# The units of an input projection in another order, and the two halves of an attention tile in one

## The chip, the cores and the metric

The kernel runs on one core of a Trainium2 chip. The metric is the device time of one execution in microseconds. Before the change three runs gave 1636.99, 1639.19 and 1640.86 us, with a median of 1639.19.

## The reference

One decoder layer is computed for two groups of requests with shared weights: a prompt of 1024 positions and 8 sample sequences of 8 positions, 1088 columns together, d_model 1024, in FP32. Cut to what matters here:

```
proj = rmsnorm(x) @ w_in        # q | k | v | glu_a | glu_b | gate_a | gate_b
A = sliding_window_attention(q, k, v) @ w_o_attn       # window 128, sinks
u = glu_a * sigmoid(glu_b)                             # 1024 channels
c = depthwise_conv(u, 31 taps) + bias
B = silu(layernorm(c)) @ w_pb
h = x + (sigmoid(gate_a) * A + sigmoid(gate_b) * B) @ w_out
y = h + conv_ffn(rmsnorm(h))
```

The change lies wholly in the second of three lines of work: the projection `proj`, the attention and the convolution `c`, which run side by side. The LayerNorm begins at their end.

## The kernel before

Activations are held with channels on the 128 partitions and the 1088 columns along the free axis, in chunks of 384, 384 and 320. FP32 products are made of three `fp32r` matmuls: each operand is split in a high part (a cast) and a low part (the rest), and `mm3` (lines 207 to 210) adds high by high, high by low and low by high. The whole stretch from 71 us to about 640 us is one long stream of such matmuls on PE.

**Units.** A unit is one tile of 128 output channels: three chunks of 8 times 3 matmuls. `SEQUENCE` (line 62) writes down their order: `b` is glu_b of the next channel tile, `a` glu_a of the same tile, `g` the next of 16 gate tiles, `q0`, `k0`, `q1`, `k1` the tiles of queries and keys for the two halves of the heads, `v` the two halves of the values (both are used in one unit of 9 blocks, 128x256 each). `weight_order` (line 92) turns it into the order in which weights are read, and `phase_x` (line 730) walks along it. The units are called below by letter and count from zero: a.7 is glu_a of the last of eight tiles, g.15 the last gate tile. The first five (b a g g g) are written apart and are the same before and after.

**Weights.** `weight` (line 196) issues the load of the raw weights two units ahead (`wraw`, on SP), and the split one unit ahead: ACT casts `whi` (L179), ACT writes its negative to `wlo` (L180), and a DMA issued by POOL (L181) adds `wraw` to `wlo`. PE's second kind of product in a unit can begin when that DMA has landed. There are two buffers of each. For `v` a third pair lies in the tile `p` of the attention pool.

**Convolution.** `do_b` takes one of two buffers `u` (`u_start`, line 747: two memsets on POOL and a small load on SP), ACT copies the chunks of glu_b there and takes the sigmoid, `do_a` has DVE multiply the chunks of glu_a into it (L774), and `conv` (line 570) runs 15 times three multiply-adds on DVE (L582), between a sum `sm` (L590) at the start and three combining operations (L602 to L604) at the end. It is issued with `later(CONV_LATER)`, a priority that puts its operations behind others that are ready. Its result goes to DRAM (`d_c`, L605 and L606, DMAs on POOL's queue), and the buffer `u` is free when they have landed.

**Attention.** After `v` and after the last `q1` unit, `plan_units` lays the steps of eight attention units and four sample units out over ticks (a tick is one k step of a unit): `scores` (L449, L450 on PE; copies, mask L454, softmax), `turn` (four transposes L461, then a split of the result in `pth` and `ptl` by ACT and DVE, L244, and two DVE multiplies by the mask, L471), and `mix` (L482 on PE with `pth`, `ptl` and their masked copies). A sample unit loads cached keys and values by DMAs on POOL's queue (`kp`, `vp`, L516 and L517).

**End of the stretch.** At the unit that stands `LAST_GATES` = 2 before the end, the agenda is drained, the pool of the attention is closed, and in its room lie `ah`, `al` (the attention's first half, six loads on SP, L1018 and L1019) and the tiles `ct` of the LayerNorm. In the last unit `ln_steps` (line 608) begins: `ct` is loaded from `d_c` for all eight channel tiles (L634), DVE sums it over the tiles (L620), and PE takes the means by a matmul with a constant (L628).

Each of SP, POOL, DVE, ACT and PE works its own instructions in the order in which the scheduler put them; the scheduler orders them when the kernel is built, by priority and by its own estimate of what is ready.

Of the kernel before, what the change touches and what calls it, by code (L numbers as in the profile page):

```python
# [6 lines left out]
F32 = mybir.dt.float32  # L7
F32R = mybir.dt.float32r
AF = mybir.ActivationFunctionType
ALU = mybir.AluOpType  # L10
AX = mybir.AxisListType

P = 128
# [12 lines left out]
WIN = 128  # L26
# [33 lines left out]
FIRST = 5  # L60
LAST_GATES = 2
SEQUENCE = (
# [3 lines left out]
).split()  # L66
OUT_TAIL = 4
LAST_WEIGHT = 153
# [61 lines left out]
class Build:  # L130
# [291 lines left out]
    def attn_unit(self, p, blk, st):  # L422
        nc = self.nc
        q, kd, kl = st["q"], st["kd"], st["kl"]
        qs = slice(blk * P, (blk + 1) * P)
        first = max(blk - 1, 0) * P
        keys = slice(first, first + 2 * WIN)
        own = slice(WIN, 2 * WIN) if blk else slice(0, WIN)
        live = [{}, {}]
        vals = {}  # L430

        def values():
            vt = vals["vt"] = self.t(self.at, [P, 2, 4, HD], "vt", F32R, bufs=2)
            self.split_ps(vt[:, 0, 0:4:3, :], vt[:, 0, 1:3, :], self.v[:, blk, p])
            if blk:
                d = self.t(self.at, [P, 2, HD], "vd")
                nc.vector.tensor_tensor(d, self.v[:, blk - 1, p], self.v[:, blk, p], ALU.subtract)
                self.split_ps(vt[:, 1, 0:4:3, :], vt[:, 1, 1:3, :], d)

        def scores(g):  # L440
            pt = live[g]["pt"] = self.t(self.at, [P, 4, WIN + 4], "p", bufs=2)
            hd = 4 * (2 * p + g)
            nc.gpsimd.tensor_copy(pt[:, :, WIN:WIN + 1], self.c("sink", hd, 4)[:, :, None])
            above = self.masks[:, 0:WIN].bitcast(mybir.dt.uint32)[:, None, :]
            for jj in range(2):
                ps = self.bank("aux").rearrange("p (a b) -> p a b", a=2)
                for j in range(2):
                    h = 2 * jj + j
                    nc.tensor.matmul(ps[:, j, :], q[g][:, h, qs], kd[g][:, keys], start=True, stop=False)  # L449
                    nc.tensor.matmul(ps[:, j, :], q[g][:, h, qs], kl[g][:, keys], start=False, stop=True)  # L450
                two = pt[:, 2 * jj:2 * jj + 2, 0:WIN]
                nc.scalar.copy(two, ps[:, :, own])
                other = ps[:, :, 0:WIN] if blk else self.least[:, None, :].to_broadcast([P, 2, WIN])
                nc.vector.copy_predicated(two, above.to_broadcast([P, 2, WIN]), other)  # L454
            self.band_softmax(pt)

        def turn(g):
            pt = live[g]["pt"]
            ps = self.bank("aux")
            for h in range(4):  # L460
                nc.tensor.transpose(ps[:, h * P:(h + 1) * P], pt[:, h, 0:P], self.ident)  # L461
            ph = self.t(self.at, [P, 512], "pth", F32R)
            pl = self.t(self.at, [P, 512], "ptl", F32R)
            parts = [(0, ph), (0, pl)]
            with self.later(TURN_SOONER if self.now - self.gated <= 3 else 0):
                self.split_ps(ph, pl, ps)
                if blk:
                    below = self.masks[:, None, WIN:2 * WIN].to_broadcast([P, 4, WIN])
                    for x, tag in ((ph, "pth0"), (pl, "ptl0")):
                        x0 = self.t(self.at, [P, 512], tag, F32R)  # L470
                        nc.vector.tensor_tensor(x0.rearrange("p (a b) -> p a b", a=4),  # L471
                                                x.bitcast(F32).rearrange("p (a b) -> p a b", a=4), below, ALU.mult)
                        parts.append((1, x0))
            live[g]["parts"] = parts

        def mix(g):
            r, o = [slice(x * HD, (x + 1) * HD) for x in (g, 1 - g)]
            av = self.bank("aux")
            parts = live[g]["parts"]
            for n, (y, x) in enumerate(parts):  # L480
                v = vals["vt"][:, y, 2 * g:2 * g + 2, :].rearrange("p x d -> p (x d)")
                nc.tensor.matmul(av, v, x, start=n == 0, stop=n == len(parts) - 1)  # L482
            if g == 0:
                live[0]["t"] = self.t(self.at, [P, 4 * P], "av").rearrange("p (a b) -> p a b", a=4)
            t = live[0]["t"]
            av = av.rearrange("p (a b) -> p a b", a=4)
            nc.scalar.copy(t[r], av[o])
            nc.vector.tensor_tensor(t[r], av[r], t[r], ALU.add)
            if g == 1:
                self.split_ps(q[0][:, :, qs], q[1][:, :, qs], t)  # L490
            if p == 0 and g == 1 and blk in (3, 7):
                b0 = (blk - 3) * P
                self.attn_spill(st, slice(b0, b0 + 4 * P))

        steps = [(A_VALUES, values)]
        for g in range(2):
            steps.append((A_SCORE[g], lambda g=g: scores(g)))
            steps.append((A_TURN[g], lambda g=g: turn(g)))
            steps.append((A_MIX[g], lambda g=g: mix(g)))
        return steps  # L500
# [229 lines left out]
    def phase_x(self):  # L730
        nc, tc, a, pool = self.nc, self.tc, self.a, self.pool
# [103 lines left out]
        def do_k(p):  # L835
            st = states[p]
            st["ks"] = self.t(kv, [P, NS], "ks")
            st["kd"] = [self.t(kv, [P, SEQ], f"kd{g}", F32R) for g in range(2)]
            st["kl"] = [self.t(kv, [P, SEQ], f"kl{g}", F32R) for g in range(2)]

            def ev(c, o, n, ps):
                m = min(n, SEQ - o)
                for g in range(2):
                    r, x = [slice(y * HD, (y + 1) * HD) for y in (g, 1 - g)]
                    kd = st["kd"][g][:, o:o + m]
                    nc.scalar.copy(kd[r], ps[r, :m])
                    kl = st["kl"][g][:, o:o + m]
                    nc.vector.tensor_tensor(kl[r], ps[r, :m], kd[r].bitcast(F32), ALU.subtract)
                    nc.scalar.copy(kd[x], ps[r, :m])
                    nc.scalar.copy(kl[x], kl[r].bitcast(F32))  # L850
                if m < n:
                    nc.scalar.copy(st["ks"], ps[:, m:n])
                    kf = self.t(gl, [P, 384], "gt", bufs=2)[:, :WIN]
                    nc.scalar.copy(kf, ps[:, m - WIN:m])
                    nc.gpsimd.dma_start(a["o_kp"][p], kf)
                    nc.gpsimd.dma_start(a["o_kn"][p], st["ks"])

            self.stream(("k", p), xs, ev)

        def do_v():  # L860
            ws = [self.weight(("v", 0)), self.weight(("v", 1))]
# [144 lines left out]
        for n, (kind, i) in enumerate(self.order[:self.n_in]):  # L1006
# [18 lines left out]
            if kind == "b":  # L1025
                u = do_b(i)
            elif kind == "a":
                do_a(i, u)
            elif kind in ("ga", "gb"):
                self.stream((kind, i), xs, gate_evac(kind, i))  # L1030
            elif kind == "q":
                if i == (1, 0):
                    self.drain()
                self.stream((kind, i), xs, q_evac(*i))
                if i == (1, 3):
                    plan_units(1)
            elif kind == "k":
                do_k(i)
            elif kind == "v":
                if i == 0:  # L1040
                    do_v()
                    plan_units(0)
# [1181 lines left out]
```

## Time and profile before

| | |
|---|---|
| profiled execution | 1639.45 us |
| its span | 1637.7 us |
| median of the runs | 1639.19 us (1636.99 to 1640.86) |
| granted TensorE clock, mean over the span | 0.998 of full speed |
| DVE, ACT, POOL busy | 84%, 55%, 18% of the span |
| ACT busy, microseconds | 901.9 |

In a row of the timeline stand the start in microseconds, the duration, the engine, the line of the kernel, the operation with its output and inputs, a count, and in square brackets how long the engine was idle ahead of it and who ended that. In a row of the waits stand the waiting engine and instruction, whom it waited for, the sum in microseconds, how often, and the longest. In a table by stretches stand, for each engine, busy microseconds and the number of instructions, then the granted TensorE clock, the busy share of the DMA engines, and GB/s. Durations of matmuls are modelled and overlap: the distance of two starts is the time that one takes.

The profile has one notable shape: PE has work nearly always, and DVE is saturated in some stages and idle in others.

### The profile page before, as it was taken

Reading aid. Unit: us, or ns where it says so; the run is one execution under the profiler, and the core shown is the slowest. Engines: PE = TensorE matmul, PEld = TensorE weight load, DVE = VectorE, ACT = ScalarE, POOL = GpSimd, SP = SyncE. Lnnn points to the kernel's source line nnn. Section 1 sums busy time; section 2 is a strip of 40 time slices with the busy share of each in tenths; the row PEclk is TensorE's granted clock in tenths of the full one; section 3 lists DMA queues with packets and bytes.
Section 4 is the critical chain, followed back from the end, with each engine's and each line's share of the span. In section 5 each row is a group of like instructions: output and inputs, shape, how many; then the busy total and the mean of one; then the engine's idle time right before and its main releaser. Section 6 shows DMA issues by size and latency. Waiting matters only on the chain.

```text
span 1637.7 us, 30023 instructions
## 1 busy us (share of the span) xinstructions
PE 1621.8 (99%) x11428; PEld 1602.6 (98%) x11428; DVE 1369.8 (84%) x2463; ACT 901.9 (55%) x1948; POOL 301.6 (18%) x587
## 2 busy tenths in 40 slices
PE   9999999999999999999999999999999999999998
PEld 9999999999999999999999999999999999999998
DVE  7889678999869996788755999988888877889767
ACT  6535387875588754576532465555555555524322
POOL 0210122333112221111102422322222111000000
PEclk9999999999999999999999999999999999999999
DMA  6343433545433366548763632344444334676423
GB/s 211 98 98 90 114 95 97 140 132 143 109 85 78 118 215 202 176 154 232 188 227 102 209 119 72 112 116 118 119 120 109 106 106 157 225 177 160 110 62 110
DMA packets 110329, 221.51 MB, mean 135 GB/s; under 512 B 26600, under 2 KB 57320, under 8 KB 110168
## 3 DMA queue, kind: packets, MB, share of 16 engines
q1 hardware_dynamic: 81528, 131.47, 26.0%
q0 software_dynamic: 28224, 87.71, 20.2%
q8 instruction: 90, 1.47, 0.4%
q14 instruction: 55, 0.45, 0.1%
q10 hardware_dynamic: 432, 0.40, 0.1%
HBM read 137.55 MB, written 64.03 MB: 123 GB/s over the span
## 4 chain that ended last, share of the span: by engine, by line
PE 80%; DVE 8%; DMA 4%; issue 4%; ACT 3%; POOL 0%; SPq 0%; POOLq 0%; DVEq 0%; ACTq 0%
PE mm L208 19%; PE mm L209 19%; PE mm L210 19%; PE aux L210 6%; PE aux L208 6%; PE aux L209 6%; DVE c L582 2%; PE aux L482 1%; DVE bt L582 1%; DVE q L824 1%; PE aux L461 1%; PE aux L449 1%; PE aux L450 1%; DMA ct<-d_c 1%; DMA wlo<-wraw 1%
## 5 line engine op out<-in xcount | busy, mean ns | idle before, releaser
L208 PE MATMUL mm<-xh,whi 128*128 128x384 f32 (+1 forms) x904 | 299.2, 331 | 0.2 <-ACT xh L297 0.2
L209 PE MATMUL mm<-xl,whi 128*128 128x384 f32 (+1 forms) x904 | 296.4, 328 | 0.4 <-DVE xl L298 0.4
L210 PE MATMUL mm<-xh,wlo 128*128 128x384 f32 (+1 forms) x904 | 296.3, 328 | 0.3 <-DMA wlo<-wraw 0.3
L209 PEld LDWEIGHTS mm<-xl,whi 128*128 128x128 f32 x904 | 170.5, 189 | 2.5 <-DVE xl L298 0.9
L208 PEld LDWEIGHTS mm<-xh,whi 128*128 128x128 f32 x904 | 170.5, 189 | 2.0 <-ACT xh L297 0.7
L210 PEld LDWEIGHTS mm<-xh,wlo 128*128 128x128 f32 x904 | 170.2, 188 | 1.1 <-DMA wlo<-wraw 0.7
L1470 DVE SCALAR_TENSOR_TENSOR acc<-st,fc,acc 128x1104 f32<-128x1104 f32 x88 | 119.8, 1364 | 12.2 <-issue 6.7
L582 DVE SCALAR_TENSOR_TENSOR bt<-u,consts,bt 128x513 f32<-128x513 f32 x120 | 89.6, 746 | 3.7 <-ACT bt L592 3.1
L210 PE MATMUL mm<-th,wlo 128*128 128x272 f32 x320 | 92.3, 289 | 0.0
L209 PE MATMUL mm<-tl,wlo 128*128 128x272 f32 x320 | 92.3, 288 | 0.0
L208 PE MATMUL mm<-th,wlo 128*128 128x272 f32 x320 | 92.2, 288 | 0.0
L582 DVE SCALAR_TENSOR_TENSOR c<-sm,hsum,c 128x512 f32<-128x512 f32 x120 | 89.3, 745 | 0.5
L210 PE MATMUL mm<-mh,wlo 128*128 128x272 f32 (+4 forms) x304 | 88.9, 292 | 0.0
L582 DVE SCALAR_TENSOR_TENSOR c<-u,consts,c 128x512 f32<-128x512 f32 x112 | 83.4, 744 | 0.4
L243 ACT CAST whi<-wraw 128x512 fp32r<-128x512 f32 x76 | 47.5, 625 | 62.7 <-PE aux L210 25.7
L1815 ACT COPY st<-mm 128x272 f32<-128x272 f32 (+2 forms) x132 | 43.5, 348 | 54.0 <-PE mm L210 53.8
L243 ACT CAST wlo<-wraw 128x512 fp32r<-128x512 f32 x76 | 47.3, 623 | 40.1 <-DVE wraw L1666 16.6
L1468 ACT ACTIVATE acc<-st,fc 128x1104 f32<-128x1104 f32 x44 | 57.6, 1315 | 14.9 <-DVE st L1771 11.8
L208 PE MATMUL aux<-mh,whi 128*128 128x272 f32 (+4 forms) x216 | 63.8, 295 | 0.0
L209 PE MATMUL aux<-ml,whi 128*128 128x272 f32 (+4 forms) x216 | 63.5, 294 | 0.0
L244 DVE TENSOR_TENSOR wlo<-wraw,wlo 128x512 fp32r<-128x512 f32 x76 | 52.7, 695 | 9.5 <-ACT wlo L243 9.3
L208 PEld LDWEIGHTS mm<-th,wlo 128*128 128x128 f32 x320 | 60.2, 188 | 0.0
(726 smaller groups left out, 5799.2 us busy)
## 6 DMA issues: line engine op xcount, KB each, us to landing
wraw<-wall SPq DMA_DIRECT2D x118, 512.0 KB, 3.8
wlo<-wraw POOLq DMA_DIRECT2D x37, 512.0 KB, 4.5
bw<-d_b SPq DMA_DIRECT2D x42, 272.0 KB, 3.9
d_b<-gd POOLq DMA_DIRECT2D x36, 272.0 KB, 6.1
d_b<-acc POOLq DMA_DIRECT2D x24, 272.0 KB, 4.7
ar<-wdn SPq DMA_DIRECT2D x32, 192.0 KB, 3.8
d_g<-acc POOLq DMA_DIRECT2D x10, 544.0 KB, 4.7
ga<-d_ga SPq DMA_DIRECT2D x8, 544.0 KB, 5.4
```

The costliest lines, as they stand in the source:

```text
L208: mm(ps, wh, xh, start=first, stop=False, skip_group_check=more)
L209: mm(ps, wh, xl, start=False, stop=False, skip_group_check=more)
L210: self.last_mm = mm(ps, wl, xh, start=False, stop=last, skip_group_check=more).ins
L243: self.cast = self.nc.scalar.copy(h, src).ins
L244: self.low = self.nc.vector.tensor_tensor(l, src, h.bitcast(F32), ALU.subtract).ins
L449: nc.tensor.matmul(ps[:, j, :], q[g][:, h, qs], kd[g][:, keys], start=True, stop=False)
L450: nc.tensor.matmul(ps[:, j, :], q[g][:, h, qs], kl[g][:, keys], start=False, stop=True)
L461: nc.tensor.transpose(ps[:, h * P:(h + 1) * P], pt[:, h, 0:P], self.ident)
L582: mac = lambda o, x, w: nc.vector.scalar_tensor_tensor(o, x, w, o, ALU.mult, ALU.add)
L1468: nc.scalar.activation(acc, st[:, 0:AW], AF.Identity, bias=fb(f), scale=fw(f, 0))
L1470: nc.vector.scalar_tensor_tensor(acc, st[:, k:k + AW], fw(f, k), acc, ALU.mult, ALU.add)
L1815: self.evicted = (add if second and n == 0 and j == 1 else op)(d, r(banks[bank, j]))
```

## The change

Three edits. First, the units come in another order: after the first query tile the second pair `b a` comes at once, and the third after two more query tiles. `k0` now stands directly ahead of `v`. Between `v` and the first `q1` stand 12 units where 11 stood, and behind the last `a` 9 gates where 7 stood. Second, in `turn` the tiles `pth` and `ptl` become the two halves of one tile `pt`, and the two mask multiplies of 512 columns become one of 1024 columns. Third, `do_k` has its unit split two weights ahead where the next unit is `v`, so that the split of both halves of `v` starts in `k0`.

```
 SEQUENCE = (
-    "b a g g g q0 q0 b a q0 q0 k0 b a v v "
-    "g b a g b a g g g b a "
-    "q1 k1 q1 q1 q1 b a g b a g g g g g g g"
+    "b a g g g q0 b a q0 q0 b a q0 k0 v v "
+    "b a g b a g b a g g b a "
+    "q1 k1 q1 q1 q1 b a g g g g g g g g g"
 ).split()
...
-            ph = self.t(self.at, [P, 512], "pth", F32R)
-            pl = self.t(self.at, [P, 512], "ptl", F32R)
-            parts = [(0, ph), (0, pl)]
+            x = self.t(self.at, [P, 2, 512], "pt", F32R)
+            parts = [(0, x[:, y]) for y in range(2)]
             with self.later(TURN_SOONER if self.now - self.gated <= 3 else 0):
-                self.split_ps(ph, pl, ps)
+                self.split_ps(x[:, 0], x[:, 1], ps)
                 if blk:
-                    below = self.masks[:, None, WIN:2 * WIN].to_broadcast([P, 4, WIN])
-                    for x, tag in ((ph, "pth0"), (pl, "ptl0")):
-                        x0 = self.t(self.at, [P, 512], tag, F32R)
-                        nc.vector.tensor_tensor(x0.rearrange("p (a b) -> p a b", a=4),
-                                                x.bitcast(F32).rearrange("p (a b) -> p a b", a=4), below, ALU.mult)
-                        parts.append((1, x0))
+                    below = self.masks[:, None, WIN:2 * WIN].to_broadcast([P, 8, WIN])
+                    x0 = self.t(self.at, [P, 2, 512], "pt0", F32R)
+                    nc.vector.tensor_tensor(x0.rearrange("p y (a b) -> p (y a) b", a=4),
+                                            x.bitcast(F32).rearrange("p y (a b) -> p (y a) b", a=4), below, ALU.mult)
+                    parts += [(1, x0[:, y]) for y in range(2)]
...
-            self.stream(("k", p), xs, ev)
+            self.stream(("k", p), xs, ev, ahead=1 + (self.order[self.w_used + 1][0] == "v"))
```

Lines behind the second edit stand two lines higher in the changed kernel (L582 becomes L580, L620 becomes L618). Three places show how instructions move.

On DVE, where the second half of the attention begins. Before, the last operation of conv 5 (L603, its output tile is `u_3956`) stands first, then the low parts of the last query tile (L824), masks, row maxima and reciprocals of the scores, and then the first split of transposed scores in that half (`ptl`):

```order
L603 TENSOR_TENSOR u_3956<-c_4226 128x512
L824 SCALAR_TENSOR_TENSOR q_508_4287<-mm_4731,q_508_4287 64x384
L824 SCALAR_TENSOR_TENSOR q_509_4288<-mm_4731,q_509_4288 64x384
L824 SCALAR_TENSOR_TENSOR q_508_4287<-mm_4760,q_508_4287 64x256
L824 SCALAR_TENSOR_TENSOR q_509_4288<-mm_4760,q_509_4288 64x256
L454 COPY_PREDICATED p_4803<-masks_889,least_84 128x2x128 x2
L414 TENSOR_REDUCE nm_4819<-p_4803 128x4
L454 COPY_PREDICATED p_4843<-masks_889,least_84 128x2x128 x2
L414 TENSOR_REDUCE nm_4859<-p_4843 128x4
L418 RECIPROCAL den_4820<-den_4820 128x4
L418 RECIPROCAL den_4860<-den_4860 128x4
L244 TENSOR_TENSOR ptl_4929<-aux_4923,pth_4928 128x512
```

After, the first two splits of that half (`pt_5034`, `pt_5069`) stand among the last operations of conv 6 (its accumulators are `c_4332`, `bt_4334`; L599 to L602 are its end):

```order
L418 RECIPROCAL den_4966<-den_4966 128x4
L580 SCALAR_TENSOR_TENSOR c_4332<-u_4136,consts_77,c_4332 128x512
L580 SCALAR_TENSOR_TENSOR c_4332<-sm_4333,hsum_87,c_4332 128x512
L580 SCALAR_TENSOR_TENSOR bt_4334<-u_4136,consts_77,bt_4334 128x513
L580 SCALAR_TENSOR_TENSOR c_4332<-sm_4333,hsum_87,c_4332 128x512
L244 TENSOR_TENSOR pt_5034<-aux_5029,pt_5034 128x512
L599 TENSOR_SCALAR u_4136<-c_4332,consts_77 128x64
L600 TENSOR_TENSOR c_4332<-c_4332,bt_4334 128x512
L602 TENSOR_TENSOR u_4136<-c_4332,bt_4334 128x512
L601 TENSOR_TENSOR u_4136<-c_4332 128x512
L244 TENSOR_TENSOR pt_5069<-aux_5064,pt_5069 128x512
```

Before, the first split has conv 5 whole ahead of it and nothing of conv 6; after, conv 6 is all but done ahead of it.

On POOL, in the stage of the first half of the attention, around the load of cached keys for the third sample unit (`kp`). Before, the low weights of the next unit (`wlo_310`, unit a.4) stand ahead of it, with one small copy between:

```order
L804 DMA d_ga_60<-gt_2938 128x320
L443 COPY p_3131<-consts_77 128x4
L181 DMA wlo_310_2948<-wraw_2744 128x1024
L443 COPY p_3184<-consts_77 128x4
L516 DMA kp_3559<-kpT 128x256
```

After, the third sample's `kp` stands directly ahead of the low weights of the next unit (`wlo_297`, unit g.4), and has a wait for PE:

```order
L181 DMA wlo_270_2743<-wraw_2531 128x1024 [waits DMAHW2_49,DMASW2_49,Activation_49]
L443 COPY p_2887<-consts_77 128x4 [waits DVE_49,PE_49]
L443 COPY p_3169<-consts_77 128x4 [waits DVE_49,PE_49]
L443 COPY p_3224<-consts_77 128x4 [waits DVE_49,PE_49]
L514 DMA kp_3527<-kpT 128x256 [waits DMASW5_49,DMASW3_49,PE_49]
L181 DMA wlo_297_2931<-wraw_2740 128x1024 [waits DMAHW3_49,DMASW4_49,Activation_49]
```

That wait is for the score matmul of the sample unit before (L519 in the changed kernel), which reads the one buffer `kp`; it stands in the last chunk of unit a.4, one chunk ahead of g.4.

On SP, at the end of the stretch. Before, two loads of raw weights and two of gate tiles `ga` stand between the loads of `ah` and `al` and the first `ct`:

```order
L1018 DMA ah_6783<-d_ah_57 128x4x384
L1019 DMA al_6784<-d_al_58 128x4x384
L1018 DMA ah_6783<-d_ah_57 128x4x320
L1019 DMA al_6784<-d_al_58 128x4x320
L157 DMA wraw_6791<-wall 128x1024
L1064 DMA ga_7020<-d_ga_60 128x1088
L1064 DMA ga_7149<-d_ga_60 128x1088
L157 DMA wraw_6882<-wall 128x1024
L634 DMA ct_6889<-d_c_59 128x8x136 x2
```

After, one load of raw weights stands between them:

```order
L1016 DMA ah_6695<-d_ah_57 128x4x384
L1017 DMA al_6696<-d_al_58 128x4x384
L1016 DMA ah_6695<-d_ah_57 128x4x320
L1017 DMA al_6696<-d_al_58 128x4x320
L157 DMA wraw_6794<-wall 128x1024
L632 DMA ct_6801<-d_c_59 128x8x136 x2
L632 DMA ct_6816<-d_c_59 128x8x136 x2
```

The loads of `ct` moved ahead of the gate tiles in the queue, and still stand behind `ah` and `al`.

## The prediction

> **What bounds the kernel now.** I read the page first, then who waited for whom on PE, then PE's and DVE's timeline at the places that the change moves, then a table of stretches, then the DMA issues. The page's row of PE, and the longest rows of its waits:
>
> ```profile
> PE 1621.8 (99%) x11428; PEld 1602.6 (98%) x11428; DVE 1369.8 (84%) x2463; ACT 901.9 (55%) x1948; POOL 301.6 (18%) x587
> ```
>
> ```profile
> PE aux L628 <- DVE sm L620: 4.7, 2, 3.4
> PE mm L209 <- DMA wlo<-wraw: 2.0, 1, 2.0
> ...
> PE aux L449 <- DVE ptl L244: 0.6, 1, 0.6
> ...
> PE mm L210 <- DMA wlo<-wraw: 0.3, 1, 0.3
> ```
>
> PE bounds the kernel; the change leaves its work as it is. What can be won are its few waits, some 7.6 us by these rows, plus what they cost behind them; what can be lost is any new wait. The two large ones in PE's timeline, the first at the start of `v`, the second inside g.15, the third (1.37 us) later in the LayerNorm:
>
> ```profile
> 177.99 0.28 PE L208 MATMUL mm<-whi,xh 128*128 128x256 f32 x1
> 180.31 0.39 PE L209 MATMUL mm<-wlo,xh 128*128 128x256 f32 x1 [2.04 <-DMA wlo<-wraw]
> 180.53 0.28 PE L210 MATMUL mm<-whi,xl 128*128 128x256 f32 x1
> 180.65 0.28 PE L208 MATMUL mm<-whi,xh 128*128 128x256 f32 x1
> ...
> 625.35 0.34 PE L210 MATMUL mm<-xh,wlo 128*128 128x384 f32 x1
> 629.05 1.24 PE L628 MATMUL aux<-sm,mean 128*128 128x272 f32 x2 [3.36 <-DVE sm L620]
> ...
> 630.62 0.47 PE L210 MATMUL mm<-xh,wlo 128*128 128x320 f32 x1
> 630.89 0.47 PE L208 MATMUL mm<-xh,whi 128*128 128x320 f32 x1
> ...
> 632.92 0.31 PE L208 MATMUL mm<-xh,whi 128*128 128x320 f32 x1
> 633.07 0.31 PE L209 MATMUL mm<-xl,whi 128*128 128x320 f32 x1
> ...
> 692.90 0.50 PE L628 MATMUL aux<-sm,mean 128*128 128x272 f32 x1 [1.37 <-DVE sm L620]
> ```
>
> Behind the 2.04 us the 256-wide matmuls follow at 0.12 us, as ever. Behind the 3.36 us the 320-wide ones follow at 0.27 us until about 632.5, then at 0.15: half rate for some 3.5 us, which loses about 1.8. So this wait is worth 3.4 + 1.8 = 5.2 us. DVE by stretches:
>
> ```profile
> core 0: us, PE busy (x) PEld busy (x) DVE busy (x) ACT busy (x) POOL busy (x), PEclk, DMA share, GB/s
> 254.00:330.00 76.00, 75.99 (x478) 73.26 (x478) 73.97 (x147) 60.57 (x169) 22.04 (x38) 1.00 0.47 123
> 332.00:442.00 110.00, 109.89 (x681) 108.53 (x681) 106.80 (x182) 65.37 (x154) 29.52 (x49) 1.00 0.48 125
> 442.00:472.00 30.00, 29.42 (x189) 28.44 (x188) 13.23 (x29) 28.90 (x82) 3.53 (x9) 1.00 0.36 92
> ...
> 590.00:613.00 23.00, 22.67 (x140) 22.34 (x139) 22.91 (x38) 8.01 (x12) 5.04 (x8) 1.00 0.91 299
> ...
> 613.00:623.00 10.00, 10.00 (x63) 10.00 (x62) 1.10 (x3) 3.87 (x5) 1.08 (x2) 1.00 0.86 285
> ```
>
> From 254 to 442 DVE is full (97%), then half idle for 30 us, then full again until conv 7 ends at 613, and from there LayerNorm hangs on conv 7. The change fills the hole with convolutions.
>
> **The change part by part.**
>
> *The wait at v.* Why it is there:
>
> ```profile
> 169.24 1.05 ACT L179 CAST p<-wraw 128x1024 fp32r<-128x1024 f32 x1 [5.29 <-DMA wraw<-wall]
> ...
> 175.08 0.87 POOL L181 DMA_DIRECT2D wlo<-wraw  x1 [2.35 <-ACT wlo L180]
> ```
>
> ACT stood 5.3 us at the cast of the second half of v, ahead of the first half's casts, whose DMA was issued at 175.08, only 5.2 us ahead of 180.31. With k0 directly ahead of v and two weights of lead, both halves are split inside k0, a unit of 24 x (0.174 + 0.174 + 0.147) = 11.9 us; POOL issues that DMA 7 to 10 us ahead of its use. The 2.04 us go, and 2.2 with the pace around them. The 0.6 and 0.3 of the list lie in the same stretch: 3.4 us of gaps in all ahead of g.15, of which I let all go, to have the new ones counted whole.
>
> *g.4's weights.* In POOL's queue `kp` now stands directly ahead of the low weights of g.4, and waits for PE in a.4's last chunk. Nearest rows:
>
> ```profile
> 280.16 0.56 POOL L516 DMA_DIRECT2D kp<-kpT  x1 [1.04 <-PE aux L521]
> ...
> wlo<-wraw POOLq DMA_DIRECT2D x37, 512.0 KB, 4.5
> ```
>
> PE's rows of a.4 and g.4, counted at the spacings above, put the score matmul's end 2.6 to 2.8 us ahead of the first use of `wlo`. Then 0.6 for `kp` and 4.5 (at most 5.2, as at v) to landing: PE waits 2.5 to 3.2 us. Bound from below: 0, if the scheduler's place for the score matmul runs earlier against PE than counted.
>
> *DVE without its hole.* The first split of the second attention half stands at the end of conv 6 in DVE's queue, and PE's mix in a.7's first chunk waits for it. What DVE has to do from the last product of a.3 to that split, against PE's way there. A convolution's 44 multiply-adds have these spacings, and the three of them with the first attention half in between took from the first row to the second:
>
> ```profile
> 254.50 0.70 DVE L590 TENSOR_TENSOR sm<-u 128x527 f32<-128x527 f32 x1
> ...
> 379.69 0.75 DVE L582 SCALAR_TENSOR_TENSOR bt<-u,consts,bt 128x513 f32<-128x513 f32 x1
> 380.35 0.74 DVE L582 SCALAR_TENSOR_TENSOR c<-u,consts,c 128x512 f32<-128x512 f32 x1
> ...
> 441.05 0.68 DVE L603 TENSOR_TENSOR u<-c 128x512 f32<-128x512 f32 x1
> ```
>
> That is 187.2 us for 328 operations; the sum of the mean spacings of their forms gives 184.9. The same sum over the 405 operations that the order after has there (a whole convolution more, 37 us, less its tail, and two more score groups and turns) gives 235.2 us. DVE can begin at 234.7: `v` starts at 177.99 in both orders (nine units behind the first q0), takes 9 x 24 x 0.12 = 25.9, b.3 and a.3 23.8, and the attention's matmuls between them 7.0. That makes 470. The bare sum fell short by 2.7 us in the stretch of the query units, which is in this path too: 472.6. PE, counted on without waits (16 units of 11.9 and 42 of attention), is at the mix at 467.1. So it comes there 5.5 us late or more; I take 6.0, between 2.8 (the bare sum) and 7.5 (the shortfall twice). g.4's wait lies inside this: PE later there leaves DVE's end where it is. Instead of 3.4 us late at g.15, PE is 6.0 late: **+2.6** (-0.6 to +4.1).
>
> *The mask multiplies.* 28 of 512 columns ahead of that split become 14 of double width:
>
> ```profile
> 472.66 0.68 DVE L471 TENSOR_TENSOR pth<-pth,masks 128x512 fp32r<-128x512 f32 x1
> 473.26 0.69 DVE L471 TENSOR_TENSOR ptl<-ptl,masks 128x512 fp32r<-128x512 f32 x1
> ...
> 1305.29 1.21 DVE L1480 TENSOR_TENSOR acc<-acc,acc 128x1024 f32<-128x1024 f32 x1
> 1306.43 0.41 DVE L244 TENSOR_TENSOR s<-wraw,s 128x256 fp32r<-128x256 f32 x1
> ```
>
> Twice 0.60 becomes 1.14: 0.06 us each, 0.8 in all, already in the sum. The first half now waits for both splits, which costs DVE nothing, as they were queued in this order.
>
> *The clock.* The new lateness comes in one or two waits: about 3 at g.4 and the rest of the 6.0 at a.7. The rows show no loss at 2.04 and 1.8 us at 3.36. I take half of one such loss, **+0.8** (0 to +3.3).
> [...]
>
> *The LayerNorm at g.15.* Conv 7 now ends long before (its inputs come two units earlier and no hole is left: by the same sums about 564 instead of 613), so the chain d_c, ct, sum is cut at its root. But the attention's second half starts one unit later, and the loads of `ah` and `al` with it, which wait for its last sample:
>
> ```profile
> 592.24 0.38 SPq L1018 DMA_DIRECT2D ah<-d_ah  x1
> ...
> 595.28 1.45 SPq L1019 DMA_DIRECT2D al<-d_al  x1
> ...
> 620.37 2.28 SPq L634 DMA_DIRECT2D ct<-d_c  x3
> ```
>
> ```profile
> GB/s 164 0 25 257 399 398 317 260 312 242 234 340 404 392 395 401 429 414 273 269 279 421 423 390 66 131 344 297 339 377 344 344 415 212 2 0 0 53 78 151
> ...
> al<-d_al SPq DMA_DIRECT2D x1, 640.0 KB, 16.8
> ```
>
> ```profile
> 627.37 0.73 DVE L620 TENSOR_TENSOR u<-ct 128x544 f32<-128x544 f32 x1 [1.24 <-DMA ct<-d_c]
> ```
>
> They took from 592.24 to 595.28 + 16.8 = 612, 20 us for two tiles of 128 x 4 x 1088 in FP32, 4.5 MB. After, their issue, behind the seventh of the nine gates, is counted 21.7 us ahead of the mean matmul. 18 to 20 us for them, 4 to 5.4 for one weight and two `ct` behind them (1.6 MB at 400 GB/s, as the best of the 40 slices from 590 to 640 have it, or at the 299 of the stretch from 590 to 613), 1.7 for DVE's sum (from its start on the last half of `ct`, 627.37, to PE's 629.05): 23.7 to 27.1, less 21.7. I take 3 us of wait, as the gate tiles that shared the queues before now stand behind; bounds 0 and 5, the latter with 1.8 of clock. Against 5.2 before: **-2.2** (-5.2 to +1.6). The 1.37 at 692.90 stays: **0** (-1.4 to +0.5).
>
> The sum: 2.6 + 0.8 - 2.2 = +1.2 us on the profiled 1639.45, which is 1640.7. The median of the runs is 0.3 lower, less than can be told.
>
> **The rivals.**
> *The waits go and none comes (faster).* For it: each wait named by the list has its cause removed, and DVE's lateness is a difference of two sums of 235 us. If DVE is on time at a.7, PE loses only g.4's wait of 2.9 against 3.4, and if `ah` and `al` move at the best slices' 400 GB/s (11 us instead of 20), g.15 loses nothing (-5.2), and the 1.37 goes: 1639.45 - 0.5 - 5.2 - 1.4 = 1632.4. Against it: the order itself shows conv 6's end around the split.
> *The queues bite with the clock (slower).* One mechanism: DVE reaches the first split later than 3.4 us against PE in one piece, and g.4's wait reaches 3.4 too. Then +4.1 instead of +2.6, two losses of 1.6, and the LayerNorm wins only 0.5, since its wait is about as long as before: 1639.45 + 4.1 + 3.2 - 0.5 = 1646.3. [...] Against it: the two waits share one lateness of 6 us, and have to be uneven or larger.
> *The early inputs are not early.* A unit b cannot leave PSUM before one of two `u` buffers is free, behind conv 3's DMA to `d_c`. If that held b.5, DVE would get conv 5 late, and the sum would be the wait at v alone: 1639.45 - 2.2 = 1637.3. Little speaks for it: the four banks cover a unit.
>
> **How the numbers follow.** A measurement of this kernel tells some 0.2% (3.3 us) from no change. Forecast 0.40, no difference that counts; faster rival 0.28; slower rival 0.28; inputs not early 0.04, which falls within the 0.2% too. So faster 0.28, same 0.44, slower 0.28. The forecast's own range, by its bounds without the extremes together, is 1637 to 1643; with both rivals, cut at a tenth each side, 1633 to 1647.
>
> **What would show it.** Right: no wait for `wlo` at the first block of v; a wait of 2.5 to 3.2 us at L210 in g.4 for `wlo`; a wait of PE for a split `pt` in a.7, the waits up to there adding to 6; DVE over 97% busy from 235 to 470; conv 7's last operation near 564; at g.15 a wait of about 3 us for the sum `sm`, with `ct` landing last behind `al`. Wrong: DVE idle for several us between 240 and 470, no wait at a.7, or no half rate and no wait at g.15, which would make it the faster case; granted clock below 1 at 287 or 470 would make it the slower one.

## The result, and the profile after

The changed kernel takes 1650.79 us (median of four runs, 1648.40 to 1651.98), the kernel before 1639.16 in the same comparison: a ratio of 1.0070, 95% interval 1.0052 to 1.0087, some 11.6 us slower. The profiled execution took 1649.94, with a span of 1648.2. So the forecast of no difference was wrong, and the time lies above the whole range, beyond even the slower rival's 1646.3.

The waits of PE after:

```profile
PE aux L626 <- DVE sm L618: 5.9, 2, 5.5
PE aux L461 <- ACT p L420: 3.8, 3, 3.3
...
PE mm L210 <- DMA wlo<-wraw: 1.0, 1, 1.0
PE mm L208 <- ACT u L762: 1.0, 1, 1.0
PE mm L208 <- DVE ml L1226: 0.9, 1, 0.9
PE aux L480 <- ACT pt L243: 0.9, 1, 0.9
PE mm L209 <- DMA wlo<-wraw: 0.8, 1, 0.8
```

Waits of about one and of three microseconds have come in new places, and the wait of the first mean (L628 before, L626 now) has grown. In PE's timeline, at v, at b.6, in b.7 and at g.15:

```profile
179.14 0.39 PE L209 MATMUL mm<-wlo,xh 128*128 128x256 f32 x1 [0.84 <-DMA wlo<-wraw]
...
390.26 0.45 PE L208 MATMUL mm<-xh,whi 128*128 128x384 f32 x1 [0.96 <-ACT u L762]
...
472.37 1.35 PE L461 MATMUL aux<-consts,p 128*128 128x128 f32 x4 [3.32 <-ACT p L420]
...
473.79 0.47 PE L209 MATMUL mm<-xl,whi 128*128 128x320 f32 x1
474.06 0.47 PE L210 MATMUL mm<-xh,wlo 128*128 128x320 f32 x1
...
640.69 1.25 PE L626 MATMUL aux<-sm,mean 128*128 128x272 f32 x2 [5.50 <-DVE sm L618]
```

Behind the waits of 3.32 and 5.50 the matmuls of 320 columns start 0.27 us apart instead of 0.147: half rate (granted clock 0.50 in both stretches), which costs about 1.5 us in b.7 (until 475.4) and 2.7 behind the mean (until 646.0; before 1.8).

| place | before, wait + half rate | after |
|---|---|---|
| v | 2.0 | 1.2 (0.84, and 0.32 for ACT) |
| first attention half, g.4 | 0 | 2.1 (0.21, 0.86, 1.00) |
| up to b.6 | 0 | 1.2 (0.23, 0.96) |
| second half's first scores | 0.6 | 3.3 + 1.5 |
| low weights at 605 | 0.3 | 0 |
| mean at g.15 | 3.4 + 1.8 | 5.5 + 2.7 |
| later | 1.4 | 1.3 (0.44, 0.9) |
| sum | 9.5 | 18.8 |

That is 9.3 of the 10.5 us between the two spans; the rest stands in no row as a wait. Two places carry most of it: 4.2 us more at the second half's first scores, 3.0 more at g.15.

**At b.7, DVE's queue.** DVE's rows there, and ACT's row for which PE waits:

```profile
467.75 0.68 DVE L414 TENSOR_REDUCE nm<-p 128x4 f32<-128x516 f32 x1
...
471.05 0.74 DVE L580 SCALAR_TENSOR_TENSOR c<-sm,hsum,c 128x512 f32<-128x512 f32 x1
471.71 0.17 DVE L418 RECIPROCAL den<-den 128x4 f32<-128x4 f32 x1
...
477.26 0.69 DVE L244 TENSOR_TENSOR pt<-aux,pt 128x512 fp32r<-128x512 f32 x1
```

```profile
471.91 1.28 ACT L420 ACTIVATE p<-p,den 128x128 f32<-128x128 f32 x4 [0.92 <-DVE den L418]
```

The reciprocal of the first scores stands between multiply-adds of conv 6. ACT scales the scores with it from 471.91, and PE's transposes begin at 472.37. The reciprocal held ACT for 0.92 us only; most of the lateness had come ahead of it, since the low parts of the last queries (L822), the mask and the row maximum (L414) of the same scores stand between multiply-adds of conv 6 too. DVE itself does not wait here; the first split follows at 477, and conv 6's end behind it.

**At g.15, SP's queue.** The loads at the end, and on DVE the end of conv 7 and the first sum of ct:

```profile
613.32 0.38 SPq L1016 DMA_DIRECT2D ah<-d_ah  x1
...
616.21 6.92 SPq L1017 DMA_DIRECT2D al<-d_al  x1
625.80 0.35 SPq L157 DMA_DIRECT2D wraw<-wall  x1
626.25 10.72 SPq L632 DMA_DIRECT2D ct<-d_c  x4
```

```profile
577.14 0.68 DVE L602 TENSOR_TENSOR u<-c,bt 128x512 f32<-128x512 f32 x1
...
637.22 0.73 DVE L618 TENSOR_TENSOR u<-ct 128x544 f32<-128x544 f32 x1 [9.05 <-DMA ct<-d_c]
```

Conv 7 had ended at 577.8, 48 us before the first `ct` was issued, which stood behind `ah`, `al` and one load of raw weights. The last load of `al` took 6.9 us to issue, that of the weights waited 2.7 more, for the buffer of raw weights that a `wlo` DMA issued at 616.76 still read.

### The profile page after: what moved, and what is told of

It is laid out like the page before. It is cut to its first block, busy times and chain, and to the rows that moved or that the text cites. A ratio compares the mean times of both kernels' runs of the same rounds, so it can differ in the third digit from the quotient of the medians.

```text
span 1648.2 us, 29989 instructions
## 1 busy us (share of the span) xinstructions
PE 1625.4 (99%) x11428; PEld 1604.6 (97%) x11428; DVE 1370.9 (83%) x2435; ACT 909.9 (55%) x1953; POOL 303.0 (18%) x587
## 4 chain that ended last, share of the span: by engine, by line
PE 83%; DVE 7%; issue 4%; DMA 3%; ACT 2%; POOL 1%; SPq 0%; POOLq 0%; ACTq 0%; DVEq 0%
PE mm L208 19%; PE mm L210 19%; PE mm L209 19%; PE aux L209 7%; PE aux L210 7%; PE aux L208 7%; DVE c L580 2%; PE aux L480 1%; DMA ct<-d_c 1%; DVE bt L580 1%; PE aux L461 1%; DVE q L822 1%; DMA wlo<-wraw 1%; PE aux L449 1%; PE aux L450 1%
## 5 line engine op out<-in xcount | busy, mean ns | idle before, releaser
L580 DVE SCALAR_TENSOR_TENSOR bt<-u,consts,bt 128x513 f32<-128x513 f32 x120 | 89.8, 748 | 0.6
L580 DVE SCALAR_TENSOR_TENSOR c<-sm,hsum,c 128x512 f32<-128x512 f32 x120 | 89.5, 746 | 0.5
L580 DVE SCALAR_TENSOR_TENSOR c<-u,consts,c 128x512 f32<-128x512 f32 x112 | 83.6, 746 | 0.6
L179 ACT CAST whi<-wraw 128x1024 fp32r<-128x1024 f32 x37 | 38.9, 1050 | 41.1 <-PE mm L209 39.8
L244 DVE TENSOR_TENSOR wlo<-wraw,wlo 128x512 fp32r<-128x512 f32 x76 | 52.9, 697 | 10.3 <-ACT wlo L243 9.6
```

The source lines that it names most:

```text
L179: self.cast = self.nc.scalar.copy(h, r).ins
L244: self.low = self.nc.vector.tensor_tensor(l, src, h.bitcast(F32), ALU.subtract).ins
L580: mac = lambda o, x, w: nc.vector.scalar_tensor_tensor(o, x, w, o, ALU.mult, ALU.add)
```

## The experiments

The theory that the profile suggests: the loss is made by the order behind v, in two places. DVE has no hole left ahead of the second attention half, so the first softmax stands in a full queue; and the loads of `ah`, `al` and `ct`, in this order, begin 12 us nearer to the mean. Rivals: the merged tile, the earlier convolutions at the front, the wait of `kp` on POOL's queue, and a plain latency of the softmax chain. All ratios are to the kernel before on the same chip.

**The merged tile alone** (`SEQUENCE` as before, second and third edit kept).

> The kernel before with the merged tile alone (second edit); the units stand in the old order, and the third edit has no effect there, as k0 does not stand directly ahead of v. Theory (the order of the units is the whole cost): no difference, 1637 to 1641 us, the waits at v, g.15 and the late mean as before. Rival (the merged tile costs: a mix needs one multiply of 1.14 us where it needed one of 0.60, which would show as many short waits in the first half of the attention): 1641 to 1643 us.

1639.27 us, ratio 1.0003 (0.9991 to 1.0014). The merged tile costs nothing that can be told. The waits at v and at the mean are 1.3 and 2.3 us, a little apart from before's.

**The new order at the front only.**

```
-    "b a g b a g b a g g b a "
-    "q1 k1 q1 q1 q1 b a g g g g g g g g g"
+    "g b a g b a g g g b a "
+    "q1 k1 q1 q1 q1 b a g b a g g g g g g g"
```

> The changed kernel with its new order only up to v; behind v the old order, with the old 11 units to q1 and 12 behind it. Theory (the cost lies in the place of the second attention half behind a full DVE, and in the loads of ah and al coming a unit later against the end): neither is there, so the time is that of before less about 1 us at v: 1637 to 1640 us, with a wait near 3 us at g.15 as before. Rival (the earlier convolutions at the front cost by filling DVE too soon): 1643 us or more.

1639.03 us, ratio 1.0003 (0.9994 to 1.0013). The waits of this kernel:

```profile
PE aux L626 <- DVE sm L618: 4.2, 2, 2.9
```

The wait at v is the changed kernel's, 0.8 us, that at g.15, 2.9, nearly the old one. The front is harmless, and its gain at v does not show in the time.

**The new order behind v only.**

```
-    "b a g g g q0 b a q0 q0 b a q0 k0 v v "
+    "b a g g g q0 q0 b a q0 q0 k0 b a v v "
```

> The changed kernel with the old order up to v and the new one behind it: 12 units to q1, 9 gates at the end. Theory: it carries nearly the whole loss: 1648 to 1653 us, with a wait of 5 us or more for the sum at g.15 and of several us in the first units of the second attention half. Rival (the front is what costs): 1640 to 1643 us.

1648.73 us, ratio 1.0063 (1.0041 to 1.0085).

```profile
PE aux L626 <- DVE sm L618: 5.4, 1, 5.4
PE aux L461 <- ACT p L420: 3.7, 3, 3.3
```

The same two waits, the same loss within the intervals: it is the order behind v.

**ct ahead of ah and al.**

```
                 self.lt = pool(a0_es, "lt")
+                w0 = T // KT
+                self.ct0 = self.t(self.lt, [P, KT, 2 * w0], "ct", bufs=2)
+                for x, o in ((0, 0), (KT // 2, w0)):
+                    nc.sync.dma_start(self.ct0[:, :, o:o + w0], self.d_c[:, :, x * w0:x * w0 + w0].rearrange("k p t -> p k t"))
...
+            if i == 0:
+                live["ct"] = self.ct0
+                return
             ct = live["ct"] = self.t(self.lt, [P, KT, 2 * n], "ct", bufs=2)
```

> The changed kernel with the first of the LayerNorm's tiles ct loaded ahead of ah and al on the same queue. Theory (the mean at g.15 waits for ct only because it stands behind ah and al, 4.5 MB): the 5.5 us wait and the half rate behind it (2.6 us) go, ct lands about 8 us behind its issue; ah and al land some 3 us later, and the output projection, which begins some 8 us sooner, waits up to 4 us for them: 1643 to 1647 us. Rival (the mean waits for DVE or for d_c, or transfers share the rate so that the order does not matter): 1649 to 1652 us.

1642.51 us, ratio 1.0021 (1.0010 to 1.0031), just under the expected range: 8 us of the 11.6 are back. The loads and the waits of this kernel:

```profile
609.06 1.64 SPq L1019 DMA_DIRECT2D ct<-d_c  x2
```

```profile
PE aux L461 <- ACT p L420: 3.7, 3, 3.3
...
PE aux L626 <- DVE sm L618: 0.6, 2, 0.3
```

The first mean, at g.15, waits for nothing instead of 5.5 us, there is no half rate behind it (granted clock 1.00 from 600 to 650), and the wait in b.7 is untouched (the two waits of up to 0.3 us are of later means). `ct` is issued at 609.06, 4 us ahead of where the changed kernel issues `ah`. `ah` follows at 615.37, and the output projection still did not wait for it: the 4 us that were allowed for that did not come. So the wait at g.15 is the order on one queue.

**Less for DVE ahead of the second half.**

```
-        for j in range(1, 16):
+        for j in range(1, 8 if i == 5 else 16):
```

> The changed kernel, with 8 of the 15 rounds of multiply-adds left out in the convolution of channel tile 5 (that tile's convolution is incomplete): 23 operations of 0.66 us, 15 us less for DVE ahead of the second attention half. Theory (PE's wait of 3.3 us in b.7 is DVE's queue: the reciprocals of the first scores stand behind conv 6's multiply-adds): the wait and the half rate behind it (1.1 us) go, the wait at g.15 stays at 5 to 6 us, as the loads of ah and al move along with PE: 1645 to 1648 us. Rival (the wait is the chain of softmax steps on ACT and DVE, whatever DVE has queued): 1650 to 1652 us.

1644.73 us, ratio 1.0033 (1.0020 to 1.0046), 6 us less than the changed kernel. This kernel's waits, and its first row maximum on DVE:

```profile
PE aux L626 <- DVE sm L618: 5.4, 1, 5.4
...
PE aux L461 <- ACT p L420: 0.4, 2, 0.2
```

```profile
463.71 0.69 DVE L414 TENSOR_REDUCE nm<-p 128x4 f32<-128x516 f32 x1
```

With 15 us less in DVE's queue the wait in b.7 is gone, and g.15 waits as in the changed kernel. The first scores come at the same time on PE (457.49, in the changed kernel 457.37); the first row maximum stands 4.0 us sooner on DVE, the reciprocal 4.8 us sooner (466.96). The chain of the softmax was not the cause; the full queue was, along the whole chain. The gain is 1 us beyond 3.3 + 1.5; the two short later waits (0.44 and 0.9) are gone as well. The two gains, 8 and 6 us, add up to more than 11.6, as the wait at g.15 cost 5.2 us in the kernel before too; no run has both.

**kp on SP's queue.**

```
-            nc.gpsimd.dma_start(kp, self.a["kpT"][p, :, 2 * bp:2 * bp + 2, :])
-            nc.gpsimd.dma_start(vp, self.a["vp"][2 * bp:2 * bp + 2, :, p * P:(p + 1) * P].rearrange("b k d -> k b d"))
+            nc.sync.dma_start(kp, self.a["kpT"][p, :, 2 * bp:2 * bp + 2, :])
+            nc.sync.dma_start(vp, self.a["vp"][2 * bp:2 * bp + 2, :, p * P:(p + 1) * P].rearrange("b k d -> k b d"))
```

> The changed kernel with the loads of cached keys and values on SP's queue instead of POOL's, so that the wait of kp for PE no longer holds the low weights of g.4. Theory: the wait of 1.0 us for wlo there goes, little else: 1648.5 to 1650.5 us. Rival (that wait only stands in for DVE's lateness, which takes it back at b.7): 1650 to 1651.5 us, with a longer wait in b.7.

1648.28 us, ratio 1.0057 (1.0042 to 1.0071), not clearly apart from the changed kernel's. The low weights in g.4, POOL's row in the changed kernel and then here:

```profile
284.29 0.56 POOL L514 DMA_DIRECT2D kp<-kpT  x1 [1.78 <-PE aux L519]
284.83 0.90 POOL L181 DMA_DIRECT2D wlo<-wraw  x1
```

```profile
284.22 0.89 POOL L181 DMA_DIRECT2D wlo<-wraw  x1 [1.72 <-ACT wlo L180]
```

Without `kp` ahead of it the DMA is issued 0.6 us sooner, and PE still waits 0.84 us for it instead of 1.00. What the DMA waits for now is ACT, which casts these weights only after the scaling of scores, and has a split between the cast and its negative. `kp` on POOL's queue had a part of it, no more.

**The first turns later.** ct first, and

```
-FIRST_UNIT = (10, 6)
-SPACING = ({"u": 22, "s": 13}, {"u": 19, "s": 13})
+FIRST_UNIT = (10, 16)
+SPACING = ({"u": 22, "s": 13}, {"u": 18, "s": 13})
```

> ct loaded first, and the turns of the second attention half's first unit 10 ticks (5 us of PE's stream) later, its units 18 ticks apart instead of 19 so that the half ends in time. Theory (in b.7 PE only has to be given 5 us of other work while DVE ends conv 6): against ct first alone the 3.3 us wait and 1.1 of half rate go: 1637 to 1640 us. Rival (DVE is the bound of the stretch, the wait comes back at a later split or mix): 1641 to 1643 us.

1646.37 us, ratio 1.0043 (1.0029 to 1.0057): the rival's mechanism, at a time 3 us above its range. The waits of this kernel:

```profile
PE aux L626 <- DVE sm L618: 3.7, 2, 1.9
PE aux L480 <- DVE pt L244: 3.4, 1, 3.4
```

The transposes no longer wait, and the mix behind them waits as long, for the split `pt` that stands in the same queue. Moving the demand by 5 us only moved the wait to the next one on DVE, and two later means then wait 1.9 us each. **With kp on SP as well**:

> The same with the loads of cached keys and values on SP's queue. Theory: 1 us less than that, 1636 to 1639 us. Rival (the stall at g.4 lies beside DVE's lateness and costs nothing of its own): the same time as without.

1643.44 us, ratio 1.0028 (1.0019 to 1.0038). 2.9 us less than without, but no less than ct first alone; neither expectation fits. In the two profiles PE's waits are 0.5 us shorter for `pt` (2.9), 1.4 for the means and 1.0 for `ml`, and only without `kp` on SP is the wait for `pt` followed by half rate (1.5 us; the mean granted clock of the span is 0.998 there, 0.999 with `kp` on SP). What of this is due to `kp` is not shown.

**One gate from between v and q1 to the end**, the rest as changed:

```
-    "b a g b a g b a g g b a "
-    "q1 k1 q1 q1 q1 b a g g g g g g g g g"
+    "b a g b a g b a g b a "
+    "q1 k1 q1 q1 q1 b a g g g g g g g g g g"
```

> The changed kernel with one gate moved from between v and the first q1 to the end (11 units between, as before; 10 gates at the end). Theory: the loads of ah, al and ct begin 12 us further from the end, so the wait at g.15 and its half rate (8.1 us) go; but DVE must do the same work ahead of the second attention half while PE comes 12 us sooner, so the waits in b.7 grow by 8 to 12 us: 1650 to 1655 us, with waits of over 10 us for the first scores or splits. Rival (the wait in b.7 is a fixed latency of 3 us): 1641 to 1644 us.

1655.67 us, ratio 1.0108 (1.0087 to 1.0128), just over the theory's range. That it comes so near is luck, as the long wait came elsewhere, and in b.7 PE waits 2.4 us, less than in the changed kernel:

```profile
PE mm L208 <- ACT u L762: 11.3, 1, 11.3
...
PE aux L626 <- DVE sm L618: 2.0, 2, 1.0
```

PE waits 11.3 us at b.6, for a bank that ACT cannot empty, since the buffer `u` is not free before conv 4 has ended on DVE and its result has left:

```profile
382.97 0.55 POOL L504 DMA_DIRECT2D d_al<-q  x1 [2.02 <-DMA d_ah<-q]
383.50 0.54 POOL L603 DMA_DIRECT2D d_c<-u  x1
...
388.50 0.12 POOL L748 MEMSET u<- 128x30 f32 x1 [3.21 <-DMA d_c<-u]
```

The changed kernel's 0.96 us at b.6 is the same wait: the two buffers `u` are the bound there. POOL's rows also show that the DMA stood behind the spill of the attention's first half. As PE was held at b.6, this run does not tell how the wait in b.7 grows. At g.15 the first mean waits for nothing, as expected from 12 us more; the two waits of 1.0 us are of later means.

**The new front, the old pairs, and one gate more at the end.**

```
-    "b a g b a g b a g g b a "
-    "q1 k1 q1 q1 q1 b a g g g g g g g g g"
+    "g b a g b a g g b a "
+    "q1 k1 q1 q1 q1 b a g b a g g g g g g g g"
```

> The new order up to v; behind it the old order with one gate moved from between v and the first q1 to the end (10 units between, 13 behind q1): g b a g b a g g b a, then q1 k1 q1 q1 q1 b a g b a and eight g. Theory (what counts is how much DVE work stands ahead of the second attention half, and how far the end is from the loads of ah, al and ct): conv 6 again comes behind the first scores, DVE's hole of 17 us before that takes up the 12 us by which PE comes sooner, and g.15 lies 12 us further from conv 7 and the loads: its wait near 3 us with the half rate goes: 1632 to 1636 us. Rival (DVE then is late at the first splits in the same way): 1640 us or more.

1650.80 us, ratio 1.0073 (1.0059 to 1.0086): missed.

```profile
PE mm L210 <- DMA wlo<-wraw: 10.8, 2, 5.7
PE aux L461 <- ACT p L420: 1.4, 2, 1.2
```

DVE and g.15 behave as the theory has it (1.2 us at the first transposes, and no wait of the first mean), but two waits for low weights, 5.7 and 5.1 us, came in their place. **With ct first**, where nothing more was to be won:

> The same with ct loaded ahead of ah and al. Theory: ct waits for conv 7 here, and ah and al stand behind it on the queue; as the waits at the end are gone already, nothing is won and up to 2 us lost: 1633 to 1638 us. Rival (ct is still late behind ah and al): 1 to 3 us less than without.

1651.19 us, ratio 1.0073 (1.0060 to 1.0086): no gain, as expected against its partner, though the level was missed with it. The rows at the two waits, POOL's and ACT's, of the former kernel:

```profile
380.97 0.54 POOL L504 DMA_DIRECT2D d_al<-q  x1 [3.04 <-DMA d_al<-q]
...
382.67 0.93 POOL L181 DMA_DIRECT2D wlo<-wraw  x1
```

```profile
619.70 1.12 ACT L1063 ACTIVATE ga<-ga 128x1088 f32<-128x1088 f32 x1 [10.33 <-DMA ga<-d_ga]
...
622.43 1.05 ACT L179 CAST whi<-wraw 128x1024 fp32r<-128x1024 f32 x1
```

Once the low weights stand behind 16 transfers of the spill on POOL, once their cast stands behind a sigmoid that waited 10.3 us for its load on ACT. **Both freed**, the last run: the spill by `nc.sync`, the first two sigmoids issued behind the last cast.

```
-            nc.gpsimd.dma_start(self.d_ah[j, :, cols], st["q"][0][:, j, cols].bitcast(F32))
-            nc.gpsimd.dma_start(self.d_al[j, :, cols], st["q"][1][:, j, cols].bitcast(F32))
+            nc.sync.dma_start(self.d_ah[j, :, cols], st["q"][0][:, j, cols].bitcast(F32))
+            nc.sync.dma_start(self.d_al[j, :, cols], st["q"][1][:, j, cols].bitcast(F32))
...
-            nc.scalar.activation(t, t, AF.Sigmoid)
+            with ExitStack() as es:
+                if m < 2:
+                    es.enter_context(tc.issue_after(self.cast))
+                nc.scalar.activation(t, t, AF.Sigmoid)
```

> The order with one gate moved to the end, and two queues freed: the spill of the attention's first half (d_ah, d_al) on SP's queue instead of POOL's, where 16 of its transfers stood ahead of the low weights of k1, and the sigmoid of the first two gate tiles ga behind the cast of the next weights on ACT, ahead of which it waited for its load. Theory (both waits of PE for wlo, 5.7 and 5.1 us, were queueing and no lack of time): they go, with their half rate of 1.5 to 1.8 us each: 1634 to 1638 us, faster than before. Rival (the weights are late anyway, as the transfers of spill, ah, al and ct share the DMA engines): 1643 to 1650 us.

1637.63 us, ratio 0.9996 (0.9988 to 1.0005). Both waits are gone, and some 13 us with them, which shows the two together to be queueing (neither was freed alone); the longest left behind the start is 2.0 us. It lies in the expected range, but is not faster: it ends level with the kernel before, and no version tried here beats that one beyond its interval.

## Why the prediction was wrong, step by step

*The wait at v* was said to go, "split inside k0", with the DMA 7 to 10 us ahead of its use. It is issued 5.2 us ahead (173.90 against 179.14), and 0.84 us stay. ACT still takes v's second half first and waits for its load:

```profile
168.52 1.05 ACT L179 CAST p<-wraw 128x1024 fp32r<-128x1024 f32 x1 [3.48 <-DMA wraw<-wall]
...
171.47 1.04 ACT L179 CAST whi<-wraw 128x1024 fp32r<-128x1024 f32 x1
```

The lead was counted from when the instruction may be issued in the program, and the load ahead of it was left out of the count. Partly right, 0.8 us mis-sized.

*g.4's weights.* 2.5 to 3.2 us were priced, 1.0 and 0.86 came, and by the run with `kp` on SP the queue named for it made only a small part. Place right, mechanism mostly wrong.

*DVE without its hole* is the step that failed in its mechanism. PE was to be 6.0 us late at the mix in a.7, for a split; it came there 11.4 us behind its count (478.52 against 467.1) and found no wait. Of the 11.4, 9.2 are the waits and the half rate of the table; the rest was not traced. Against the kernel before, PE's first matmul on `ah` began 11.7 us later (646.37 against 634.68). Less the 3.0 of the mean, 8.7 us were lost ahead of it, where 2.6 and 0.8 for the clock had been forecast. Two errors. The first split ended at 477.95 and not at 472.6: DVE began 1.0 us later than counted and then stood idle 5.5 us in short waits, 1.3 us of it for ACT's sigmoid of `u`, the rest for steps of the attention on ACT, against 2.2 in before's stretch with which the sum was compared. (The shortfall taken twice gives 8.2 and not 7.5 for the upper bound; that is too low as well.) And the split against the mix was the wrong pair: ten rows ahead of it in DVE's queue stands the first reciprocal, ahead of that the mask and the maximum of the same scores, and PE asks for what follows from them at the transposes in b.7, some 5 us before the mix. PE was held there. The run with turns moved shows both pairs at work, and the short convolution shows that DVE's queue is the cause. That DVE would be full was right: 96% from 235 to 470 us.

*The clock.* One half of a loss was taken, 0.8; before's rows have 1.8 for a whole one, and the 1.6 for each loss in the slower rival's sum stands in none. In b.7 a whole loss was 1.5; the loss behind the mean grew by 0.9.

*The mask multiplies* cost nothing, by the run with the merged tile alone; the 0.8 us that they were to save is too little to be seen in it.

*The LayerNorm* was to win 2.2 us and lost 3.0, a miss of 5.2, as large as that ahead of it. The lead was counted rightly: `ah` was issued at 613.32, 21.7 us ahead of 635.0, where the mean was due. What was priced too low is what it had to wait for: 23.9 us from there to the first sum of `ct`, and 3.5 more for the second half and DVE's sums. The step added rates of transfer, took the lower end, and left out that the load of weights between `al` and `ct` has a wait of its own on SP's queue (2.7 us). Conv 7 ended 13.8 us later than the 564 of the count, without effect, as `ct` was issued 48 us behind it.

*The rivals.* The slower one named the right kind of thing, queues with half rate behind them, and had g.4 for one of its two places, which was wrong; its 1646.3 lacked the wait that grew at g.15. The 3.4 us that each of its two waits was to reach is the length of before's wait at g.15 (3.36); no run shows it as a limit, and 2.38 us were enough in the run with the gate at the end. That the inputs are held by their buffers, given 0.04 because "the four banks cover a unit", did happen, for 0.96 us at b.6 and for 11.3 in the run with the gate at the end.

## What to carry to other kernels

Where an engine works its instructions in order and is full, every row in its queue that another engine needs has to be compared with the time at which that engine asks, along the whole chain and not only at the most visible row; the earliest pair decides, and giving it slack uncovers the next (3.3 us at the transposes, then 3.4 at the mix). Loads that are wanted first belong first in their queue: one whose data had been made 48 us earlier waited for 4.5 MB that PE needed only 30 us later, and moving it won 8 us. An order of units that fills one engine's hole (DVE was busy for 13.2 of the 30 us from 442 to 472 before, for 29.3 after) takes away the slack in which the others' queues were late without harm.

## What the runs showed of the hardware

Before the change, PE kept its rate behind a wait of 2.04 us (matmuls of 256 columns 0.12 us apart, granted clock 1.00 from 180.3 to 182.5) and ran at half rate behind one of 3.36 (320 columns 0.27 us apart, granted clock 0.51 from 629.5 to 632.5). The experiments do not bear out a limit between the two. In b.7 a wait of 2.77 us in the run with `kp` on SP, and one of 2.38 us in the first run with a gate moved to the end, were followed by half rate (320 columns 0.27 us apart instead of 0.147; the granted clock of the second was 0.94 over 450 to 480), while one of 2.93 us in the run that moved the turns and `kp` was not (384 columns 0.17 apart, granted clock 1.00 from 480 to 500). The second and the third:

```profile
472.38 1.35 PE L461 MATMUL aux<-consts,p 128*128 128x128 f32 x4 [2.38 <-ACT p L420]
...
473.79 0.47 PE L209 MATMUL mm<-xl,whi 128*128 128x320 f32 x1
474.06 0.47 PE L210 MATMUL mm<-xh,wlo 128*128 128x320 f32 x1
```

```profile
481.64 0.74 PE L480 MATMUL aux<-pt,vt 128*128 128x512 f32 x2 [2.93 <-DVE pt L244]
482.22 0.34 PE L208 MATMUL mm<-xh,whi 128*128 128x384 f32 x1
482.39 0.34 PE L209 MATMUL mm<-xl,whi 128*128 128x384 f32 x1
```

Two short waits close together were followed by it too. At g.4, in the run with the new order behind v only, PE waited 0.86 us at 286.70 and 1.05 us at 288.96, and then ran at half rate for 3.3 us (384 columns 0.32 us apart instead of 0.17, granted clock 0.98 over 290 to 350):

```profile
288.96 0.69 PE L210 MATMUL mm<-xh,wlo 128*128 128x384 f32 x1 [1.05 <-DMA wlo<-wraw]
289.45 0.52 PE L208 MATMUL mm<-xh,whi 128*128 128x384 f32 x1
289.77 0.52 PE L209 MATMUL mm<-xl,whi 128*128 128x384 f32 x1
```

With `ct` first the same happened behind 0.86 and 0.97 us (0.32 us apart); in the changed kernel, behind 0.86 and 1.00, the granted clock stayed at 1.00 (from 286 to 292). So the length of a wait does not tell by itself whether the rate is lost; what decides is not shown.
